# Three blocks of the second merge gate moved ahead of a recurrence's readout, and the readout's quarters queued on TensorE behind named products

## The chip, the cores and the metric

One core of one Trainium2 chip runs the whole kernel in one launch. The metric is the device time of an execution in microseconds (us). Below, TensorE is PE (PEld its weight loads), VectorE is DVE, ScalarE is ACT, GpSimd is POOL and SyncE is SP; ACTq and SPq are the streams that ACT and SP issue their DMAs from.

## What is computed

One layer of a decoder trunk on 256 tokens of width 2048, in float32: a gated feed-forward layer, a mixer, and a second feed-forward layer, each between two norms. Only the mixer matters here. Cut down, with the names of the reference:

```
proj = u @ W_in                        # u: 256 x 2048; columns split into u_ssm, q, k/v, gates, g_a, g_b
bu   = einsum(u_ssm, B)                # 64 groups of 16 channels, 64 complex states each
x[t] = A * x[t-1] + bu[t]              # a linear recurrence over the tokens
y    = Re(C x) + D u_ssm               # its readout
y_A  = (gelu(y) @ W1) * sigmoid(gelu(y) @ W2)
y_B  = NSA(q, k, v) @ W_o              # attention: compressed, selected and windowed branch
h    = h + post((sigmoid(g_a) * y_A + sigmoid(g_b) * y_B) @ W_out)
```

## The kernel before

All large products run through one routine, `block`. It makes a 256 x 512 piece of a product in two PSUM accumulators (`acc`, one for each half `t` of the tokens; two pairs exist). The weights come as a stream of items of 512 KB (two slices of 128 rows by 512 columns), loaded by SP's DMAs into `raw`, and each item is split by ACT (L88, the high part `hi`) and DVE (L89, the low part `lo`), at most four items ahead of their use. For each slice and each half, three matmuls follow: hi x high part of the activations (L185), lo x high (L186), hi x low (L187). A block with 2048 rows has 8 items and 96 products. After each item a block calls `tick`, which by `pump` takes one entry off the list `background` and traces it there, so that other work is woven between the products.

The order on each engine is that in which the tile framework's scheduler puts the traced instructions when the kernel is built: among those that can go it prefers the earlier traced one. On the chip each engine works through its own list in that order, and waits where an operand isn't there. Buffers that share a tag (`wk`, thirteen of 128 x 512; `xp`, four PSUM tiles; `tab`, two; `four`, four) are handed out in the order in which the trace asks for them.

The mixer (L635 on) runs, in this order: two blocks for the recurrence's input (transposed into `urel`); a block for keys, one for values, one for the compressed branch's inputs; three narrower blocks for the queries (twice 384 columns, then 304 with the attention's gates, L769); the four blocks of the gate g_b in the order of `GATE_ORDER` (L969), whose sigmoids go by ACT (L963) and SP's DMAs to `sig_dram`, but for the last; then, four times, a block of g_a and two half-length blocks on `yth`/`ytl` (L983 to L990); then the attention's output product (L1011, from `qs`) and W_out.

The recurrence advances four tokens a step, 64 steps. `s5_in` (L685) makes its inputs on PE; `scan` (L693) does the steps on POOL, four instructions each (L698 to L701), each needing the one before it; `s5_out` (L705) reads the states out on PE, for two of eight channel groups at a time a quarter (two calls, 48 matmuls, L713), each call with a table of 768 KB loaded by ACT's DMA queue (L682). The readout needs the states of all 64 steps. `s5_gelu` (L718) takes a quarter through ACT and DVE (L721, L730 to L734), four PE transposes (L226) and on to `yth`/`ytl` (L726, L727). These entries go onto `background` in this order: eight `s5_in`, sixteen `scan` of four steps, and for each quarter two `s5_out` and one `s5_gelu`. The ticks of the key, value and compressed blocks (8 each) take the first 24, and those of the query blocks the rest. When the query blocks are traced, what is left of the list is pumped (L781), the recurrence's pool `ssm` is closed, and the attention's pool `nsa` is opened in its place: its first DMAs (`tb` L788, `pos` L795, `w2c` L797, from ACT's queue) go there. The attention puts 57 entries on the list (L943 to L956), which the ticks from the first block of g_b on take.

Of the kernel before, what the change touches and what calls it, by code (L numbers as in the profile page):

```python
# [12 lines left out]
AF = mybir.ActivationFunctionType  # L13
# [7 lines left out]
NT = 2  # L21
KD = D // 128
# [10 lines left out]
ACC_BUFS = 4  # L33
LAG = 3
GATE_ORDER = (1, 2, 3, 0)
OPENING = [(0, 0), 1, 2, (0, 1), (1, 0), 3, (0, 2), (1, 1), 4, (0, 3), (1, 2), (1, 3)]
ORDER = {3: 1, 4: 2, 5: 3}
MAGIC = 12582912.0
# [66 lines left out]
def body(tc, a):  # L105
    from contextlib import ExitStack, nullcontext

    nc = tc.nc
    V, S, G, T = nc.vector, nc.scalar, nc.gpsimd, nc.tensor
# [9 lines left out]
    def work(dt=F32):  # L119
        return wk.tile([128, 512], dt, name="wk", tag="wk")  # L120
# [42 lines left out]
    nc.scalar.dma_start(gains, a["gains"])  # L163
    for x in OPENING:
        if isinstance(x, tuple):
# [4 lines left out]
    background = []  # L170

    def pump(n=1):
        for _ in range(n):
            if background:
                background.pop(0)()

    def block(lhs, nk, width=512, tick=None, held=0, between=None, behind=None, lag=0):
        acc = [ps.tile([128, 512], F32, name="acc", tag="acc") for _ in range(NT)]

        def products(parts, kk, t):  # L180
            wh, wl = parts
            for k in range(wh.shape[1]):
                lh, ll = lhs(t, kk + k)
                o = acc[t][:, :width]
                T.matmul(o, lh, wh[:, k, :], start=kk + k == 0, stop=False)  # L185
                T.matmul(o, lh, wl[:, k, :], start=False, stop=False)  # L186
                T.matmul(o, ll, wh[:, k, :], start=False, stop=kk + k == nk - 1)  # L187

        kk = 0
        kept = []  # L190
        late = []
        while kk < nk:
            parts = stream.next()
            products(parts, kk, 0)
            if kk < nk - held:
                late.append((parts, kk))
                if len(late) > lag:
                    products(*late.pop(0), 1)
            else:
                kept.append((parts, kk))  # L200
                if late:
                    products(*late.pop(0), 1)
            kk += parts[0].shape[1]
            if tick is not None:
                tick(kk)
        for x in late:
            products(*x, 1)
        if held:
            if between is not None:
                between(acc)  # L210
            for n, (parts, k0) in enumerate(kept):
                ins = behind(n) if behind is not None else None
                with tc.issue_after(ins) if ins is not None else nullcontext():
                    products(parts, k0, 1)
        return acc
# [7 lines left out]
    def transpose4(src, cols=128, n=4):  # L223
        p = xp.tile([128, n, 128], F32, name="xp", tag="xp")
        for k in range(n):
            last_transpose[0] = T.transpose(p[:, k, :], src[:, k * cols:(k + 1) * cols], ident).ins  # L226
        return p

    last_transpose = [None]


    act_h = [None] * NT
# [399 lines left out]
    sig_dram = dp.tile([256, D - 512], F32, name="sig")  # L632


    def mixer(name, rr, gen, post, last):  # L635
# [31 lines left out]
        for b in range(2):  # L667
            acc = acc0 if b == 0 else block(act, KD)
            for t in range(NT):
                p = transpose4(natural(acc, t))  # L670
                for q in range(4):
                    x = p[32 * q:32 * q + 32].rearrange("p c (n j) -> p c j n", j=4)
                    for j in range(4):
                        o = urel[32 * j:32 * j + 32, 4 * b:4 * b + 4, q, 32 * t:32 * t + 32]
# [5 lines left out]
        def table(src, n):  # L680
            w = sm.tile([128, 1536], F32, name="tab", tag="tab", bufs=2)
            nc.scalar.dma_start(w[:, :n], src)  # L682
            return w
# [9 lines left out]
        def scan(n0, n1):  # L693
            for n in range(n0, n1):
                w = sm.tile([128, 2, 2, 32], F32, name="sc", tag="sc", bufs=2)
                x = st8[:, :, :, n]
                y = st8[:, :, :, n + 1]
                G.tensor_tensor(w[:, 0], x, a4r2, op=ALU.mult)  # L698
                G.tensor_tensor(w[:, 1], x[:, ::-1], a4i2, op=ALU.mult)  # L699
                G.tensor_tensor(y, y, w[:, 0], op=ALU.add)  # L700
                G.tensor_tensor(y, y, w[:, 1], op=ALU.add)  # L701
# [3 lines left out]
        def s5_out(ct):  # L705
            tab = table(out_dram[ct], 1536).rearrange("p (r q k) -> p r q k", r=3, q=4)
            if ct % 2 == 0:
                yps.append(xp.tile([128, 2, 2, 128], F32, name="xp", tag="xp"))
            for qh in range(2):
                for r in range(3):  # L710
                    for q2 in range(2):
                        q = 2 * qh + q2
                        T.matmul(yps[-1][64 * q2:64 * q2 + 64, ct % 2, qh, :],  # L713
                                 st8[:, r, 4 * ct + q, 0:64] if r < 2 else urel[:, ct, q, :],
                                 tab[:, r, q, :], start=r == 0, stop=r == 2, tile_position=(0, 64 * q2))


        def s5_gelu(cp2):  # L718
            yp = yps.pop(0)
            yw, y2 = work(), work()  # L720
            S.activation(yw, yp.rearrange("p a b (i c) -> p i a b c", i=4), AF.Copy)  # L721
            gelu2(yw, y2)
            p = transpose4(yw).rearrange("p i (q n) -> p i q n", q=2)
            ks = slice(2 * cp2, 2 * cp2 + 2)
            oh, ol = (x[:, ks].rearrange("p q (n i) -> p i q n", i=4) for x in (yth, ytl))
            S.activation(oh, p, AF.Copy, scale=0.5)  # L726
            V.scalar_tensor_tensor(ol, p, 0.5, oh.bitcast(F32), op0=ALU.mult, op1=ALU.subtract)  # L727

        def gelu2(y, t):
            S.activation(t, y, AF.Square)  # L730
            V.tensor_scalar(t, t, GELU_C * 0.044715, GELU_C, op0=ALU.mult, op1=ALU.add)
            V.tensor_tensor(t, t, y, op=ALU.mult)
            S.activation(t, t, AF.Tanh)
            V.scalar_tensor_tensor(y, t, 1.0, y, op0=ALU.add, op1=ALU.mult)  # L734
# [2 lines left out]
            background.append(lambda ct=ct: s5_in(ct))  # L737
        for n0 in range(0, 64, 4):
            background.append(lambda n0=n0: scan(n0, n0 + 4))
        for ct in range(8):  # L740
            background.append(lambda ct=ct: s5_out(ct))
            if ct % 2:
                background.append(lambda ct=ct: s5_gelu(ct // 2))


        acc = block(act, KD, tick=tick)
# [21 lines left out]
        rh = [rr_half(rr(t), f"rh{t}") for t in range(NT)]  # L768
        for p0, np_, width in ((0, 3, 384), (3, 3, 384), (6, 2, 304)):  # L769
            acc = block(act, KD, width=width, tick=tick)  # L770
            for t in range(NT):
                p = transpose4(natural(acc, t, 128 * np_), n=np_)
                for hf in range(2):
                    own, other = (slice(64 * o, 64 * o + 64) for o in (hf, 1 - hf))
                    qh, ql = (qs[o, p0:p0 + np_, hf, t * 128:(t + 1) * 128] for o in (own, other))
                    S.activation(qh, p[own], AF.Copy, scale=-0.125)
                    V.scalar_tensor_tensor(ql, p[own], -0.125, qh.bitcast(F32), op0=ALU.mult, op1=ALU.subtract)
                if width == 304:
                    S.activation(gates[t], acc[t][:, 256:304], AF.Tanh, scale=rh[t])
                    V.tensor_scalar(gates[t], gates[t], 0.5, 0.5, op0=ALU.mult, op1=ALU.add)  # L780
        pump(len(background))  # L781
        ssm.__exit__(None, None, None)

# [172 lines left out]
                background.append(lambda u=units[i - 1]: values(*u))  # L956


        def gate(ab_acc):
            sg = []  # L960
            for t in range(NT):
                sg.append(work())
                S.activation(sg[t], ab_acc[t], AF.Tanh, scale=rh[t])  # L963
            return sg

        def sig_place(nb, t):
            return sig_dram[t * 128:(t + 1) * 128, (nb - 1) * 512:nb * 512]

        for nb in GATE_ORDER:  # L969
            sg_b = gate(block(act, KD, tick=tick))  # L970
            if nb:
                for t in range(NT):
                    nc.sync.dma_start(sig_place(nb, t), sg_b[t])

        def ylhs(t, kk):
            return yth[:, kk, t * 128:(t + 1) * 128], ytl[:, kk, t * 128:(t + 1) * 128]
# [5 lines left out]
        for nb in range(NBD):  # L982
            sg = gate(block(act, KD, tick=tick))  # L983
# [20 lines left out]
        for nb in range(NBD):  # L1004
            if nb:
                sg_b = []
# [3 lines left out]
            sg, w2 = sg_b, ya[nb]  # L1010
# [17 lines left out]
    def rr_half(r, nm):  # L1028
        h = cp.tile([128, 1], F32, name=nm, tag=nm)
        V.tensor_scalar(h, r, 0.5, None, op0=ALU.mult)  # L1030
        return h
# [57 lines left out]
def layout(i):  # L1089
# [19 lines left out]
    d["w_qg"] = _tiles(np.concatenate([q[:, 768:], gn], axis=1), 304)  # L1109
    d["w_gate_b"] = _tiles(np.concatenate([gb[:, nb * 512:(nb + 1) * 512] for nb in GATE_ORDER], axis=1))  # L1110
    wo = f["nsa_w_o"].reshape(16, 64, D)[heads].reshape(1024, D)
# [33 lines left out]
```

## Time and profile before

| | |
|---|---|
| median of 3 runs | 2211.38 us (2211.06 to 2211.67) |
| the profiled execution | 2210.69 us |
| its span in the trace | 2208.9 us |
| PE busy | 2145.2 us, 97% |
| DVE, ACT, POOL busy | 54%, 45%, 11% |
| mean granted PE clock | 0.987 of full |

Times in the trace are us from the start of the span. "Idle before" is the time in which the engine sat idle ahead of an instruction, with what released it behind the arrow. Matmuls are pipelined, so that the pace of a run of products is read from the distance of their starts, not from the length of one. POOL's records are rough: the last step of the recurrence is recorded as ending some 1.4 us after the matmul that needed it had begun.

### The profile page before, as it was taken

Reading aid. Unit: us, or ns where it says so; the run is one execution under the profiler, and the core shown is the slowest. Engines: PE = TensorE matmul, PEld = TensorE weight load, DVE = VectorE, ACT = ScalarE, POOL = GpSimd, SP = SyncE. Lnnn points to the kernel's source line nnn. Section 1 sums busy time; section 2 is a strip of 40 time slices with the busy share of each in tenths; the row PEclk is TensorE's granted clock in tenths of the full one; section 3 lists DMA queues with packets and bytes.
Section 4 is the critical chain, followed back from the end, with each engine's and each line's share of the span. In section 5 each row is a group of like instructions: output and inputs, shape, how many; then the busy total and the mean of one; then the engine's idle time right before and its main releaser. Section 6 shows DMA issues by size and latency. Waiting matters only on the chain.

```text
span 2208.9 us, 27461 instructions
## 1 busy us (share of the span) xinstructions
PE 2145.2 (97%) x10246; PEld 1772.9 (80%) x10246; DVE 1197.5 (54%) x1674; ACT 998.5 (45%) x1347; POOL 249.1 (11%) x494
## 2 busy tenths in 40 slices
PE   8999999999999999659999999999999999999998
PEld 7888888888888888647877788888888888888887
DVE  7877745544444654324555546574455444544444
ACT  6444444444444654324455444473444444444442
POOL 1222210000000006931044200000000000000000
PEclk9999999999999999869999999999999999999999
DMA  8777766666666766437533456575656665666664
GB/s 290 255 235 234 228 190 191 190 190 195 197 199 218 249 210 195 127 116 267 191 127 130 145 191 223 195 261 190 190 190 190 191 191 190 190 191 199 198 215 161
DMA packets 137141, 437.60 MB, mean 198 GB/s; under 512 B 14880, under 2 KB 27312, under 8 KB 136880
## 3 DMA queue, kind: packets, MB, share of 16 engines
q1 hardware_dynamic: 117504, 403.10, 56.4%
q10 hardware_dynamic: 19504, 32.75, 4.4%
q8 instruction: 80, 1.31, 0.2%
q14 instruction: 53, 0.43, 0.1%
HBM read 417.42 MB, written 21.52 MB: 199 GB/s over the span
## 4 chain that ended last, share of the span: by engine, by line
PE 93%; POOL 5%; issue 1%; DMA 0%; ACT 0%; ACTq 0%; DVE 0%; DVEq 0%; SPq 0%; POOLq 0%
PE acc L185 29%; PE acc L187 29%; PE acc L186 29%; PE xp L226 2%; POOL sc L698 1%; POOL sc L699 1%; POOL st L701 1%; POOL st L700 1%; PE xp L937 1%; PE xp L713 1%; PE xp L690 1%; PE xp L925 1%; PE xp L826 0%; PE xp L901 0%; PE xp L931 0%
## 5 line engine op out<-in xcount | busy, mean ns | idle before, releaser
L89 DVE TENSOR_TENSOR lo<-raw,hi 128x1024 fp32r<-128x1024 f32 (+2 forms) x702 | 854.6, 1219 | 844.8 <-ACT hi L88 836.7
L88 ACT ACTIVATE hi<-raw 128x1024 fp32r<-128x1024 f32 (+2 forms) x702 | 737.5, 1052 | 993.3 <-PE acc L187 933.0
L185 PE MATMUL acc<-hi,ah 128*128 128x512 f32 (+2 forms) x1968 | 764.2, 390 | 7.6 <-ACT wk L657 6.2
L186 PE MATMUL acc<-lo,ah 128*128 128x512 f32 (+2 forms) x1968 | 763.1, 388 | 0.0
L187 PE MATMUL acc<-hi,al 128*128 128x512 f32 (+2 forms) x1968 | 762.8, 388 | 0.0
L185 PEld LDWEIGHTS acc<-hi,ah 128*128 128x128 f32 x1968 | 370.9, 189 | 83.1 <-ACT wk L657 6.7
L187 PEld LDWEIGHTS acc<-hi,al 128*128 128x128 f32 x1968 | 370.9, 188 | 74.2 <-issue 1.3
L186 PEld LDWEIGHTS acc<-lo,ah 128*128 128x128 f32 x1968 | 371.2, 189 | 72.3 <-issue 1.3
L187 PE MATMUL acc<-hi,hT 128*128 128x512 f32 x648 | 252.1, 389 | 0.0
L186 PE MATMUL acc<-lo,hT 128*128 128x512 f32 x648 | 252.1, 389 | 0.0
L185 PE MATMUL acc<-hi,hT 128*128 128x512 f32 x648 | 251.9, 389 | 0.0
L185 PEld LDWEIGHTS acc<-hi,hT 128*128 128x128 f32 x648 | 121.7, 188 | 25.2
L187 PEld LDWEIGHTS acc<-hi,hT 128*128 128x128 f32 x648 | 121.7, 188 | 25.2
L186 PEld LDWEIGHTS acc<-lo,hT 128*128 128x128 f32 x648 | 121.7, 188 | 25.1
L302 POOL TENSOR_TENSOR rpc<-rpc,mhalf 128x1 f32<-128x1 f32 x2 | 1.1, 548 | 719.5 <-DVE rpc L300 719.5
L588 POOL COPY hz<-hs 32x128 f32<-32x128 f32 (+3 forms) x128 | 58.7, 459 | 183.3 <-DVE hs L583 176.3
L912 POOL TENSOR_SCALAR four<-four,sx 128x128 f32<-128x128 f32 (+1 forms) x64 | 59.2, 943 | 123.7 <-ACT four L907 65.2
L226 PE MATMUL xp<-ident,wk 128*128 128x128 f32 x368 | 51.0, 278 | 9.0 <-DMA wk<-in_x 4.9
L226 PEld LDWEIGHTS xp<-ident,wk 128*128 128x128 f32 x368 | 44.3, 143 | 16.0 <-issue 9.1
L302 POOL TENSOR_TENSOR rpa<-rpa,mhalf 128x1 f32<-128x1 f32 x2 | 1.1, 554 | 468.5 <-DVE rpa L300 468.5
L713 PE MATMUL xp<-tab,st 128*64 128x128 f32 x128 | 12.5, 327 | 39.6 <-POOL st L701 39.6
L185 PE MATMUL acc<-hi,yth 128*128 128x512 f32 x128 | 50.3, 393 | 0.0
(264 smaller groups left out, 1544.0 us busy)
## 6 DMA issues: line engine op xcount, KB each, us to landing
raw<-in_ffn_gu SPq DMA_DIRECT2D x352, 512.0 KB, 3.6
raw<-in_ffn_d SPq DMA_DIRECT2D x176, 512.0 KB, 3.6
raw<-in_w_ya SPq DMA_DIRECT2D x64, 512.0 KB, 3.5
raw<-in_w_in SPq DMA_DIRECT2D x40, 512.0 KB, 4.6
raw<-in_w_gate_b SPq DMA_DIRECT2D x32, 512.0 KB, 4.1
raw<-in_w_out SPq DMA_DIRECT2D x32, 512.0 KB, 4.3
raw<-in_w_o SPq DMA_DIRECT2D x16, 512.0 KB, 4.2
tab<-s5out ACTq DMA_DIRECT2D x8, 768.0 KB, 5.5
```

The lines of the kernel that those rows point to most:

```text
L88: self.rounded.append(nc.scalar.activation(h, r, AF.Copy).ins)
L89: nc.vector.tensor_tensor(l, r, h.bitcast(F32), op=ALU.subtract)
L185: T.matmul(o, lh, wh[:, k, :], start=kk + k == 0, stop=False)
L186: T.matmul(o, lh, wl[:, k, :], start=False, stop=False)
L187: T.matmul(o, ll, wh[:, k, :], start=False, stop=kk + k == nk - 1)
L226: last_transpose[0] = T.transpose(p[:, k, :], src[:, k * cols:(k + 1) * cols], ident).ins
L588: G.tensor_copy(hq[32 * j:32 * j + 32, q, j:, :], hs[32 * q:32 * q + 32, 0:4 - j, :])
L690: T.matmul(sp[:, r, q, :], bt[:, r, q, :], urel[:, ct, q, :], start=True, stop=True)
L698: G.tensor_tensor(w[:, 0], x, a4r2, op=ALU.mult)
L699: G.tensor_tensor(w[:, 1], x[:, ::-1], a4i2, op=ALU.mult)
L713: T.matmul(yps[-1][64 * q2:64 * q2 + 64, ct % 2, qh, :], st8[:, r, 4 * ct + q, 0:64] if r < 2 else urel[:, ct, q, :], tab[:, r, q, :], sta ...
L912: G.tensor_scalar(P[:, b, :nk], P[:, b, :nk], sx[:, 2 + b:3 + b], None, op0=ALU.mult)
```

## The change

A constant `EARLY_GATES = 3` is added. `gate` and `sig_place` are moved up, unaltered, and a routine `gate_b` does a block of g_b with its sigmoid and its stores. The first three blocks of g_b (nb = 1, 2, 3) are traced right behind the query blocks, ahead of the last pump and the closing of `ssm`; the fourth (nb = 0) stays where all four stood, and is the first whose ticks take the attention's entries. The weights' order in the stream is the same.

The readout isn't put on the list together with the scan. Ahead of the third block of g_b the list is emptied, and eight entries go onto it: readout of a quarter, gelu of that quarter, four times. The third block's eight ticks take them. Each readout is traced under `issue_after(last_product[0])`: its PE instructions may not stand on PE ahead of the latest L187 product traced by then (`block` now keeps it in `last_product`), that is the last product of items 1, 3, 5 and 7 of the third block.

```diff
+EARLY_GATES = 3
@@ block, products
-                T.matmul(o, ll, wh[:, k, :], start=False, stop=kk + k == nk - 1)
+                last_product[0] = T.matmul(o, ll, wh[:, k, :], start=False, stop=kk + k == nk - 1).ins
@@ mixer, background of the recurrence
-        for ct in range(8):
-            background.append(lambda ct=ct: s5_out(ct))
-            if ct % 2:
-                background.append(lambda ct=ct: s5_gelu(ct // 2))
+        def readout(c2):
+            with tc.issue_after(last_product[0]):
+                for ct in (2 * c2, 2 * c2 + 1):
+                    s5_out(ct)
@@ mixer, behind the query blocks
+        def gate_b(nb):
+            sg = gate(block(act, KD, tick=tick))
+            if nb:
+                for t in range(NT):
+                    nc.sync.dma_start(sig_place(nb, t), sg[t])
+            return sg
+
+        for i, nb in enumerate(GATE_ORDER[:EARLY_GATES]):
+            if i == EARLY_GATES - 1:
+                pump(len(background))
+                for c2 in range(4):
+                    background.append(lambda c2=c2: readout(c2))
+                    background.append(lambda c2=c2: s5_gelu(c2))
+            gate_b(nb)
         pump(len(background))
         ssm.__exit__(None, None, None)
@@ mixer, behind the attention's entries
-        for nb in GATE_ORDER:
-            sg_b = gate(block(act, KD, tick=tick))
-            if nb:
-                for t in range(NT):
-                    nc.sync.dma_start(sig_place(nb, t), sg_b[t])
+        for nb in GATE_ORDER[EARLY_GATES:]:
+            sg_b = gate_b(nb)
```

## Rows read from the trace of the kernel before

**Rows 1.** The page: busy time by engine, PE's granted clock in 40 slices of 55.2 us (tenths of full speed), and the engines' shares of the chain that ended last.
```profile
PE 2145.2 (97%) x10246; PEld 1772.9 (80%) x10246; DVE 1197.5 (54%) x1674; ACT 998.5 (45%) x1347; POOL 249.1 (11%) x494
...
PEclk9999999999999999869999999999999999999999
...
PE 93%; POOL 5%; issue 1%; DMA 0%; ACT 0%; ACTq 0%; DVE 0%; DVEq 0%; SPq 0%; POOLq 0%
```

**Rows 2.** PE's waits of the whole span (what waited, for whom: total us, times, longest us); the two that are left out belong to the start of the kernel (4.9) and to a weight split (1.4).
```profile
PE xp L713 <- POOL st L701: 39.6, 1, 39.6
PE acc L185 <- ACT wk L657: 6.2, 2, 4.4
...
PE xp L226 <- DVE wk L734: 4.0, 1, 4.0
```

**Rows 3.** The timeline of PE from the second query block's last product on, merged (start, us, instruction, idle before): the first three readout quarters (L713), transposes (L226), the third query block (L185). Between 975.91 and 981.30 stand 27 recorded products.
```profile
920.04 0.34 PE L187 MATMUL acc<-hi,al 128*128 128x384 f32 x1
959.97 1.12 PE L713 MATMUL xp<-tab,st 128*64 128x128 f32 x8 [39.59 <-POOL st L701]
...
968.32 1.09 PE L226 MATMUL xp<-ident,wk 128*128 128x128 f32 x4 [4.03 <-DVE wk L734]
969.33 1.12 PE L713 MATMUL xp<-tab,st 128*64 128x128 f32 x8
...
975.91 0.41 PE L185 MATMUL acc<-hi,ah 128*128 128x304 f32 x1 [1.83 <-ACT wk L657]
...
981.30 0.60 PE L226 MATMUL xp<-ident,wk 128*128 128x128 f32 x4
981.83 0.66 PE L713 MATMUL xp<-tab,st 128*64 128x128 f32 x8
...
984.61 0.87 PE L226 MATMUL xp<-ident,wk 128*128 128x128 f32 x6
```

**Rows 4.** Windows of that stretch and behind it: busy us of PE, PEld, DVE, ACT, POOL, then the granted clock, the DMA share and GB/s.
```profile
960.00:980.00 20.00, 14.14 (x118) 13.36 (x119) 4.71 (x7) 5.75 (x9) 1.31 (x4) 0.67 0.47 158
1000.00:1005.00 5.00, 2.16 (x5) 1.78 (x6) 1.49 (x4) 3.31 (x8) 0.00 (x0) 0.56 1.06 354
```

**Rows 5.** Starts of PE's products: two of 512 columns with 36 steps between them, two of 304 columns with 13 steps between them, and two of 512 columns next to each other in the first g_b block.
```profile
1083.15 0.40 PE L185 MATMUL acc<-hi,ah 128*128 128x512 f32 x1
...
1091.33 0.39 PE L185 MATMUL acc<-hi,ah 128*128 128x512 f32 x1
...
988.10 0.30 PE L187 MATMUL acc<-hi,al 128*128 128x304 f32 x1
...
989.91 0.30 PE L185 MATMUL acc<-hi,ah 128*128 128x304 f32 x1
...
1006.42 0.63 PE L187 MATMUL acc<-hi,al 128*128 128x512 f32 x1
1006.85 0.63 PE L185 MATMUL acc<-hi,ah 128*128 128x512 f32 x1
```

**Rows 6.** Windows for the last instruction of a scan step alone (L701 on POOL): its busy us and, behind x, how many steps; then the granted clock, the DMA share and GB/s. The scan begins at 842, the second query block ends at 920.2.
```profile
842.00:886.00 44.00, 9.80 (x20) 1.00 0.58 187
842.00:920.20 78.20, 15.53 (x36) 1.00 0.57 179
903.60:920.20 16.60, 2.87 (x8) 1.00 0.54 158
```

**Rows 7.** The timelines of POOL and of DVE: a scan instruction beside a weight split (L89), and the scan's last two steps, with DVE idle.
```profile
868.29 1.42 POOL L701 TENSOR_TENSOR st<-st,sc 128x64 f32<-128x64 f32 x1
...
868.26 1.22 DVE L89 TENSOR_TENSOR lo<-raw,hi 128x1024 fp32r<-128x1024 f32 x1 [0.90 <-ACT hi L88]
...
959.56 0.35 POOL L701 TENSOR_TENSOR st<-st,sc 128x64 f32<-128x64 f32 x1
...
961.03 0.35 POOL L701 TENSOR_TENSOR st<-st,sc 128x64 f32<-128x64 f32 x1
```

**Rows 8.** The sixteen DMAs that load the recurrence's tables (L682), us from issue to landing; and a window of what follows the readout (columns as in rows 4).
```profile
DMA to landing us min/median/max: 4.3/4.9/8.4
...
1000.00:1040.00 40.00, 37.16 (x171) 28.57 (x172) 19.90 (x24) 19.83 (x30) 4.85 (x2) 0.91 0.81 269
```

**Rows 9.** The timeline of ACT and of its DMA queue: the second quarter's gelu (L721, L730, L726; L733 is of the same form and length as L730) with the first query block's L657 behind its L730, and the second of the attention's first DMAs; and the group of the weight splits on ACT (busy us, mean ns of one).
```profile
974.13 0.60 ACT L721 ACTIVATE wk<-xp 128x512 f32<-128x512 f32 x1 [3.60 <-PE xp L713]
...
974.76 0.63 ACT L730 ACTIVATE wk<-wk 128x512 f32<-128x512 f32 x1
975.30 1.04 ACT L657 ACTIVATE wk<-acc,rna 128x384 f32<-128x384 f32 x2
...
981.98 1.11 ACT L726 ACTIVATE yth<-xp 128x512 fp32r<-128x512 f32 x1
...
997.41 4.22 ACTq L795 DMA_DIRECT2D pos<-in_cmp_pos  x1
...
L88 ACT ACTIVATE hi<-raw 128x1024 fp32r<-128x1024 f32 (+2 forms) x702 | 737.5, 1052 | 993.3 <-PE acc L187 933.0 <-issue 16.4 <-POOL hz L588 11.8
```

**Rows 10.** The attention's last result, the first product that reads the attention's results, and a window of the attention's busiest stretch (columns as in rows 4).
```profile
1255.59 0.29 DVE L941 TENSOR_TENSOR qs<-xp,qs 128x128 fp32r<-128x128 f32 x1 [0.38 <-ACT qs L940]
...
1335.53 0.39 PE L185 MATMUL acc<-hi,qs 128*128 128x512 f32 x1
...
1150.00:1200.00 50.00, 50.00 (x291) 38.02 (x287) 30.00 (x97) 27.43 (x69) 19.51 (x22) 1.00 0.36 127
```

More of the change, by code (lines that the diff above doesn't have):

```diff
@@ L229, in body @@
     last_transpose = [None]
+    last_product = [None]
     act_h = [None] * NT
@@ L780, in mixer, with gate, sig_place @@
                     V.tensor_scalar(gates[t], gates[t], 0.5, 0.5, op0=ALU.mult, op1=ALU.add)
+        def gate(ab_acc):
+            sg = []
+            for t in range(NT):
+                sg.append(work())
+                S.activation(sg[t], ab_acc[t], AF.Tanh, scale=rh[t])
+            return sg
+        def sig_place(nb, t):
+            return sig_dram[t * 128:(t + 1) * 128, (nb - 1) * 512:nb * 512]
+        def gate_b(nb):
+            sg = gate(block(act, KD, tick=tick))
+            if nb:
+                for t in range(NT):
+                    nc.sync.dma_start(sig_place(nb, t), sg[t])
+            return sg
+        for i, nb in enumerate(GATE_ORDER[:EARLY_GATES]):
[5 more added lines that the diff above has]
+            gate_b(nb)
         pump(len(background))
@@ L956, in mixer @@
                 background.append(lambda u=units[i - 1]: values(*u))
-        def gate(ab_acc):
-            sg = []
-            for t in range(NT):
[L962 to L967, printed above, removed]
-        for nb in GATE_ORDER:
-            sg_b = gate(block(act, KD, tick=tick))
-            if nb:
-                for t in range(NT):
-                    nc.sync.dma_start(sig_place(nb, t), sg_b[t])
+        for nb in GATE_ORDER[EARLY_GATES:]:
+            sg_b = gate_b(nb)
         def ylhs(t, kk):
```

## The prediction, made before the changed kernel was run

> **What bounds the kernel now.** I read the page first. PE is busy for 97% of the span, so that the kernel is the sum of PE's work and PE's waits; no other engine passes 54%. Its granted clock is lower in two slices in the middle, and the chain that ended last has 5% of POOL, an engine that is busy for only 11% [rows 1]. The list of PE's waits names the place: one wait of 39.6 us for the recurrence's last step on POOL, 6.2 us for ACT in two, 4.0 us for DVE in one; the rest is small and elsewhere [rows 2]. The timeline of PE puts these into one stretch behind the query blocks [rows 3]. The reader should see there that the 48 matmuls of the first readout quarter stand on PE right behind the second query block, while the third query block, which needs nothing of the recurrence, stands behind two quarters. It needs the accumulators of the first query block, these are emptied by ACT's L657, and that stands on ACT behind the first steps of the gelu of two quarters [rows 9], since the `wk` buffers are handed out in trace order. So what the third query block could have covered is locked behind the readout as well.
>
> **What the stretch costs.** From the end of the second query block (920.2: the last product starts at 920.04) PE idles 39.59 + 4.03 [rows 3] + 6.2 [rows 2] = 49.8 us. On top comes a granted clock of 0.67 in the window from 960 to 980 and of 0.56 at 1000 to 1005 [rows 4], so half speed (1.2 GHz) for part of them, after PE had been idle. What it costs I take from work of the same kind at both speeds. A quarter at full speed takes 2.78 us (the third: 981.83 to 984.61); the first took 4.32 (959.97 to 964.29, where the 4.03 us of waiting begin), the second 4.75 (969.33 to 974.08, where the 1.83 begin): 1.54 + 1.97. Four transposes took 1.01 instead of 0.53: 0.48 [rows 3]. A product of 512 columns takes (1091.33 - 1083.15) / 36 = 0.227 us, one of 304 columns (989.91 - 988.10) / 13 = 0.139 us [rows 5]; the 27 products from 975.91 to 981.30 [rows 3] took 5.39 instead of 3.75: 1.64. In the first g_b block some ten products took 0.43 [rows 5]: with a slow start, 2.2. Together 7.8 us. **The stretch holds 49.8 + 7.8 = 57.6 us that are not work.**
>
> **Part 1: three blocks go ahead.** They add nothing: the same 96 products each, in the same order of the stream. What they do is give PE work that needs no state of the recurrence: 96 x 0.227 = 21.8 us each. The third query block (96 x 0.139 = 13.4 us) is freed too, because the gelu no longer stands ahead of L657 on ACT. With the 16 transposes of the query blocks (at 0.53 / 4, 2.1 us) the first readout quarter, behind the third gate block's first item (12 products, 2.7 us), comes up on PE at 920.2 + 13.4 + 2.1 + 2 x 21.8 + 2.7 = **982.0 us** at the earliest.
>
> When is the recurrence done by then? Before, its last steps ran while DVE stood still, at 961.03 - 959.56 = 1.47 us each. Now DVE will be splitting weights all through, and that is dearer: a scan instruction of 0.35 us takes 1.42 when it meets an L89 of 1.22 [rows 7], and in the blocks of 512 columns 20 steps took 44 us, 2.2 each [rows 6]. By the row, 36 steps are done at 920.2 [rows 6], 28 remain, and 28 x 2.2 = 61.6 puts the end at 981.8 in POOL's records. These run 1.4 us late against PE's (the last step ends at 961.38, the matmul that needed it began at 959.97) [rows 3, 7]: 980.4. **The cover is nearly exact: 1.6 us to spare.** The fastest loaded pace (16.6 / 8 = 2.08) gives 977 and no wait; the slowest, with the count of a window of 22 us with ten steps one too high at its edges (22 / 9 = 2.44), gives 987 and a wait of 5 us, after which the clock falls as it did after 4.4 us of idling (2.2 us more). I take 0 for this wait, since the 512-wide blocks are the nearest rows, with 0 to 7 us as bounds.
>
> The Trainium skill (GPSIMD Engine Reference, 1. Specifications) states that GpSimd's SBUF interfaces are shared with VectorE, with contention for DVE instructions with two SBUF inputs, which L89 is; that speaks against this change. The trace agrees, at 1.42 against 0.35 us [rows 7]. Without such a rule the scan would be over at 960 as before, and the change would have 22 us to spare instead of 1.6; the sum would be the same.
>
> **Part 2: the quarters are spread over the third block.** PE's work in them is the same (4 x 2.78 us). What is new is what each can wait for. A quarter's tables need the buffers of the quarter before it: 768 KB each, 4.3 to 8.4 us to landing, median 4.9 [rows 8], issued from ACT's queue when half of the quarter before is done. Two items and four transposes lie between: the second quarter begins 2.8 + 5.4 + 0.5 = 8.7 us after the first, and its first table lands at some 1.4 + 0.6 + 4.9 = 6.9, at the longest 10.4, a wait of 1.7. For three quarters: 0 to 5 us; I take 1, since the tables now share the DMA engines with a full stream of weights. The third block moves 4.2 MB of weights and 4.7 MB of tables in 21.8 + 4 x 2.8 + 3 x 0.5 = 34.5 us, 258 GB/s, and the trace has 269 over 40 us [rows 8] and 354 over 5 [rows 4]: SP's weights don't fall behind. ACT has 8 x 1.05 of splits and 4 x 2.97 of gelu (0.60 + 2 x 0.63 + 1.11) [rows 9], 20 of 34.5 us; the sigmoids and the DMA issues fit beside them. The gelu of a quarter takes 4.0 us when nothing else runs (what the first transposes waited) [rows 3]; products now lie between, but ACT and DVE are also busy with splits: 0 to 2 us for each of four, I take 0.5 in all. Going back and forth between products and other matmuls: 0.5 us more than before.
>
> The sigmoid of the third block stands on ACT behind the last gelu's L730, because `wk` is handed out in order. Waiting for it are two accumulators, which the block after next needs 22 us later, and SP's stores with the weight loads behind them; up to five raw items and four split ones are ahead. Nothing.
>
> **Part 3: the attention starts later.** Its DMAs wait for the last quarter. The 4.2 us in which ACT sat on the issue of `pos` [rows 9] come again, but now behind the third block: no accumulators that PE needs at once hang on it, and PE has up to four split items (2.7 us each) in hand. Nothing, up to 2 us. The 57 entries have only 8 + 64 ticks. Before, `pos` was issued at 997.4 and the attention's last result stood at 1255.9, 258.5 us later; the product that reads it began at 1335.5 [rows 9, 10]. Now the last quarter ends at some 979.3 (the third block's start) + 19.1 (seven items) + 11.1 (four quarters) + 1.6 (transposes) = 1011.1, the attention at some 1270.2, and PE arrives at its output product at 1335.5 - 55.6 = 1280; the last heads are needed by the fourth item, 8 us later. The cover shrinks from 80 us to 10 (18 for the last heads), but it holds.
>
> **Sum.** 57.6 - (0 + 1 + 0.5 + 0.5) = 55.6 us. The profiled execution took 2210.69 (its span of 2208.9 and 1.8 around it), which gives 2155.1; it lies 0.7 under the median, which gives 2211.38 - 55.6 = 2155.8: **2156 us.**
>
> **The rivals.**
>
> *The scan outlasts the cover.* For it: the margin is 1.6 us of 62. Then PE waits at the third block for POOL for 3 to 6 us, and the clock takes 2 more: 2159 to 2164.
>
> *The readout's chain is slower than its spacing.* Each quarter waits for tables and gelu, the scheduler puts later quarters into the fourth block, the attention ends behind 1288, and PE waits at its output product. The price is what the attention is late, less the 18 us; a chain of 20 us a quarter instead of 8.7 delays the last quarter by 3 x 11.3 = 34 and costs 16, less with waits of only a few us at the quarters: 2159 to 2172.
>
> *It doesn't do what it says.* `issue_after` sets only the earliest place on PE. If something that the readout holds still locks PE's next work behind it on ACT, only the wait for POOL goes: 2211.4 - 39.6 = 2172.
>
> *Slower.* The attention becomes the bound of the mixer. Its 57 entries share their ticks with the g_a blocks, where ACT and DVE have the sigmoid products besides. It decides from an end of the attention 18 us behind its forecast, and the change loses from 18 + 55.6 = 74 us on: 258.5 us would have to become 332 or more. At 340 us the time is 2219. Against it: DVE is at 60% and ACT at 55% in its busiest stretch [rows 10], and what the g_a blocks add is small.
>
> **Chances.** Forecast (2152 to 2159) 0.60; scan outlasts 0.16; chain 0.12; not what it says 0.07; slower 0.03, and 0.02 for about the same. The range reaches from 2151, a stretch with nothing new and some 2 us of order that falls well elsewhere, to 2172, which leaves out less than 0.1. Changes under 0.2% (4.4 us) can't be told from none in this kernel: faster 0.95, same 0.02, slower 0.03.
>
> **What would show it.** Right: PE's waits have no line for POOL above 2 us; the granted clock is 1.0 from 900 to 1020; the quarters are a few us apart, with products between, and begin at some 982; the scan's steps take 2.2 us up to its end at about 981; the attention's last result comes before 1280. Wrong: a wait L713 <- POOL of over 3 us (the cover's pace is off), L713 <- DMA or L226 <- DVE of over 3 us in sum (part 2), a wait of the first product on `qs` (part 3), or L185 <- ACT L657 still there (the lock).

## The result and the profile after

| | before | changed |
|---|---|---|
| median | 2211.53 us | 2154.77 us (2154.32 to 2155.35) |
| ratio to before, 95% interval | | 0.9742 [0.9725, 0.9759] |
| span of the profiled execution | 2208.9 us | 2153.0 us |
| mean granted PE clock | 0.987 | 0.999 |

The change saves 55.9 us of the profiled executions' span (forecast: 55.6) and 56.8 us between the medians, 2.6% of the time. Lines of the changed kernel are numbered a little higher: the readout is L716 (L713 before), the last instruction of a scan step L704 (L701), the DVE split L91 (L89), the accumulator's L657 is L660, the attention's last result L970 (L941), the transposes L228 (L226), ACT's split L90 (L88), and the three products L187 to L189 (L185 to L187).

The page of the changed kernel, to be held against [rows 1]:

```profile
PE 2137.8 (99%) x10246; PEld 1765.6 (82%) x10246; DVE 1201.0 (56%) x1674; ACT 998.4 (46%) x1347; POOL 273.2 (13%) x494
...
PEclk9999999999999999999999999999999999999999
```

PE has the same 10246 instructions. Its busy time is 7.4 us less: the granted clock is full in every slice, and the half clock had added this to the same instructions (7.8 in the prediction). And the span less the busy time fell from 63.7 to 15.2 us. POOL is busy 24 us longer with the same 494 instructions: the scan is now loaded to its end. All of PE's waits of the whole span, against [rows 2]:

```profile
PE xp L228 <- DMA wk<-in_x: 5.2, 2, 4.9
PE acc L187 <- ACT hi L90: 1.6, 2, 1.4
PE xp L716 <- POOL st L704: 0.9, 1, 0.9
```

What is left is the start of the kernel (4.9 of the 5.2 us), a weight split and 0.9 us for the scan. The timeline of PE, merged, around the first readout quarter and ahead of the second to the fourth, against [rows 3]:

```profile
981.80 0.39 PE L189 MATMUL acc<-hi,al 128*128 128x512 f32 x1
983.11 0.66 PE L716 MATMUL xp<-tab,st 128*64 128x128 f32 x8 [0.92 <-POOL st L704]
...
994.64 0.60 PE L228 MATMUL xp<-ident,wk 128*128 128x128 f32 x4
995.16 0.66 PE L716 MATMUL xp<-tab,st 128*64 128x128 f32 x8
...
1008.37 0.66 PE L716 MATMUL xp<-tab,st 128*64 128x128 f32 x8
...
1020.66 0.66 PE L716 MATMUL xp<-tab,st 128*64 128x128 f32 x8
```

The reader should see two things. The first quarter came up at 983.11 - 0.92 = 982.2 (forecast 982.0), with the scan some 1 us behind it (forecast: 1.6 ahead). And the quarters are 12 to 13 us apart, not 8.7; between them PE does products without a wait. The windows for L704 show the scan's pace under the gate blocks (behind x the steps), against [rows 6]:

```profile
920.00:940.00 20.00, 3.66 (x9) 1.00 0.75 241
940.00:960.00 20.00, 5.13 (x9) 1.00 0.64 213
960.00:980.00 20.00, 4.77 (x8) 1.00 0.64 213
```

26 steps in 60 us are 2.3 us a step; in the last two rows of [rows 7] it was 1.47 with DVE idle.

The attention's last result and the first product that reads it, as first and last start of their groups (the sixteen L970; L187 on `qs`), against [rows 10]:

```profile
L970 DVE TENSOR_TENSOR qs<-xp,qs x16: 269/284/292, 1140.3 to 1273.8; 128x128 fp32r<-128x128 f32 x16
...
L187 PE MATMUL acc<-hi,qs x64: 389/389/476, 1279.6 to 1325.1; 128*128 128x512 f32 x64
```

The attention ends 5.5 us ahead of its reader (80 before; forecast 10).

### The profile page after: what moved, and what is told of

Its sections match the earlier page's. It is cut to its first block, busy times and chain, and to the rows that moved or that the text cites. A ratio compares the mean times of both kernels' runs of the same rounds, so it can differ in the third digit from the quotient of the medians.

```text
span 2153.0 us, 27454 instructions
## 1 busy us (share of the span) xinstructions
PE 2137.8 (99%) x10246; PEld 1765.6 (82%) x10246; DVE 1201.0 (56%) x1674; ACT 998.4 (46%) x1347; POOL 273.2 (13%) x494
## 4 chain that ended last, share of the span: by engine, by line
PE 91%; POOL 6%; issue 1%; DMA 1%; DVE 1%; ACT 0%; DVEq 0%; SPq 0%; ACTq 0%; POOLq 0%
PE acc L187 28%; PE acc L188 28%; PE acc L189 28%; PE xp L228 2%; POOL sc L701 2%; POOL st L704 2%; POOL st L703 1%; POOL sc L702 1%; PE xp L966 1%; PE xp L693 1%; PE xp L954 1%; PE xp L716 1%; PE xp L855 0%; DMA s5out<-gb 0%; PE xp L930 0%
## 5 line engine op out<-in xcount | busy, mean ns | idle before, releaser
L91 DVE TENSOR_TENSOR lo<-raw,hi 128x1024 fp32r<-128x1024 f32 (+2 forms) x702 | 858.8, 1224 | 822.9 <-ACT hi L90 813.2
L90 ACT ACTIVATE hi<-raw 128x1024 fp32r<-128x1024 f32 (+2 forms) x702 | 737.5, 1052 | 970.8 <-PE acc L189 907.4
L187 PE MATMUL acc<-hi,ah 128*128 128x512 f32 (+2 forms) x1968 | 762.7, 389 | 1.6 <-ACT hi L90 1.6
L189 PE MATMUL acc<-hi,al 128*128 128x512 f32 (+2 forms) x1968 | 761.3, 387 | 0.0
L187 PEld LDWEIGHTS acc<-hi,ah 128*128 128x128 f32 x1968 | 369.8, 188 | 77.7 <-issue 3.6
L189 PEld LDWEIGHTS acc<-hi,al 128*128 128x128 f32 x1968 | 369.8, 188 | 72.8 <-issue 0.2
L189 PE MATMUL acc<-hi,hT 128*128 128x512 f32 x648 | 252.1, 389 | 0.0
L187 PE MATMUL acc<-hi,hT 128*128 128x512 f32 x648 | 251.9, 389 | 0.0
L189 PEld LDWEIGHTS acc<-hi,hT 128*128 128x128 f32 x648 | 121.6, 188 | 25.3
L187 PEld LDWEIGHTS acc<-hi,hT 128*128 128x128 f32 x648 | 121.6, 188 | 25.1
L941 POOL TENSOR_SCALAR four<-four,sx 128x128 f32<-128x128 f32 (+1 forms) x64 | 59.3, 944 | 122.7 <-ACT four L936 59.3
L228 PE MATMUL xp<-ident,wk 128*128 128x128 f32 x368 | 51.1, 276 | 5.2 <-DMA wk<-in_x 5.2
L228 PEld LDWEIGHTS xp<-ident,wk 128*128 128x128 f32 x368 | 44.4, 143 | 12.3 <-issue 4.9
L187 PE MATMUL acc<-hi,yth 128*128 128x512 f32 x128 | 50.6, 395 | 0.0
L189 PE MATMUL acc<-hi,ytl 128*128 128x512 f32 x128 | 50.5, 395 | 0.0
```

Of the source, the lines that this page charges most:

```text
L90: self.rounded.append(nc.scalar.activation(h, r, AF.Copy).ins)
L91: nc.vector.tensor_tensor(l, r, h.bitcast(F32), op=ALU.subtract)
L189: last_product[0] = T.matmul(o, ll, wh[:, k, :], start=False, stop=kk + k == nk - 1).ins
L941: G.tensor_scalar(P[:, b, :nk], P[:, b, :nk], sx[:, 2 + b:3 + b], None, op0=ALU.mult)
```

## The experiments

The theory to be tested: the 57.6 us hang on the scan's late end and on the lock of the `wk` order, and on nothing else; the three g_b blocks are cover, counted in PE time; the scan's pace, which the cover has to outlast, is set by DVE's splits. The main rivals: the moving of the gates, or the naming of products, does the work by itself; or part of the loss stands on its own.

### One part alone: the gates moved, the readout left on the list

```diff
-        def readout(c2): ...                       # and its entries ahead of the third block
+        for ct in range(8):                        # directly behind the scan's entries, as before
+            background.append(lambda ct=ct: s5_out(ct))
+            if ct % 2:
+                background.append(lambda ct=ct: s5_gelu(ct // 2))
```

> The three g_b blocks are moved up, but the readout and gelu entries stay on the list directly behind the scan, as before. My theory (the query blocks' and gates' accumulators hang on wk buffers that are handed out behind the gelu, so that whatever stands behind the readout in the trace is locked): the first quarter stands behind the second query block again, PE waits some 39.6 us for POOL, and the time is 2211 +- 4 us. Rival (moving the gates up is enough, since they need nothing of the recurrence and can fill the wait): 2155 to 2175 us.

Measured: 2213.25 us, ratio 1.0006 [0.9997, 1.0015]. PE's waits are those of [rows 2] again:

```profile
PE xp L716 <- POOL st L704: 39.5, 1, 39.5
PE acc L187 <- ACT wk L660: 6.1, 2, 4.3
...
PE xp L228 <- DVE wk L737: 4.0, 1, 4.0
```

Three blocks that need nothing of the recurrence stood earlier in the program and moved nothing. They were traced ahead of the attention, but still behind the readout, whose entries the query blocks' ticks take, and the waits for ACT's L660 (L657 before) are there as before. Moving the gates is not enough; where the readout is traced decides.

### The other part alone: the readout traced last, no gate moved

The kernel before, with the readout and the gelu traced right behind the third query block.

```diff
-        for ct in range(8):
-            background.append(lambda ct=ct: s5_out(ct)) ...
         pump(len(background))
+        for c2 in range(4):
+            s5_out(2 * c2)
+            s5_out(2 * c2 + 1)
+            s5_gelu(c2)
         ssm.__exit__(None, None, None)
```

> The kernel before, with the readout and the gelu taken off the list and traced right behind the third query block; no g_b block is moved. This takes away the lock (the first query block's L657 no longer stands behind the gelu) and nothing else. My theory: PE does the third query block first and comes to the first quarter at some 936 us, with 21 scan steps to go: a wait of some 30 us, 2185 to 2200. Rival (the lock was the whole cause: once it is gone the scheduler fills the wait with g_b blocks, which need nothing of the recurrence): 2155 to 2170.

Measured: 2182.17 us, ratio 0.9864 [0.9849, 0.9878]. The timeline of PE:

```profile
941.31 0.39 PE L187 MATMUL acc<-hi,al 128*128 128x512 f32 x1
...
967.51 1.12 PE L713 MATMUL xp<-tab,st 128*64 128x128 f32 x8 [25.82 <-POOL st L701]
```

Taking the lock away is worth some 30 us: the third query block, and the first 30 recorded products of the first g_b block, which the scheduler put ahead by itself, now stand before the wait; the waits for L657 and L734 are gone. The rest, 2182.2 - 2154.8 = 27 us, is a wait of 25.8 us and the clock behind it, which needs more cover or an earlier end of the scan. The time is 3 us below the range that I gave; the 30 products (30 x 0.227 = 6.8 us), which I had left to the rival, are more than that.

### The same with half of the scan

As the last kernel, but 32 of the 64 scan steps are left out (`range(0, 32, 4)`).

> The kernel before with the readout traced behind the third query block (no lock) and with 32 of the 64 scan steps left out; no g_b block is moved and nothing is tied to a product. The scan ends at some 907 us, well ahead of the place that the trace order gives to the first quarter (some 936). My theory (the lost 57.6 us come from the late scan and the lock alone; the g_b blocks that the change moves are cover and nothing else): no wait of PE for POOL, a granted clock of 1.0 throughout, 2153 to 2158 us. Rival (part of the loss stands by itself: ACT's issue of pos, the gelu ahead of the transposes, and moving the gates is what hides it): 2160 to 2172 us.

Measured: 2154.36 us, ratio 0.9741 [0.9724, 0.9757], the time of the changed kernel, without any of its moved gates. The kernel before took 2211.78 us beside it: 57.4 us more, against the 57.6 us that the prediction counted. PE's waits, complete:

```profile
PE xp L226 <- DMA wk<-in_x: 5.0, 1, 5.0
PE acc L185 <- ACT hi L88: 1.4, 1, 1.4
```

So no loss of a size that can be measured stood by itself. Where the scan ends in time and the order holds no lock, the g_b blocks may stay where they were.

### Half of the scan in the kernel before, as it was

```diff
-        for n0 in range(0, 64, 4):
+        for n0 in range(0, 32, 4):
```

> The kernel before, with 32 of the 64 scan steps left out. The scan would then end at some 842 + 32 x 2.2 = 912 us, ahead of the place of the first quarter. My theory (all that the stretch lost came from the late end of the scan, the waits for ACT and DVE and the clock with it): 2152 to 2160 us, like the changed kernel, with at most the 4.4 us of ACT's issue of pos left. Rival (the scan's wait is one loss among several that stand by themselves): only the 39.6 us go, 2172 us.

Measured: 2173.98 us, ratio 0.9828 [0.9813, 0.9843]: near the rival's number, but not for its reason, and my expectation failed. With eight entries fewer on the list the readout's entries moved forward by eight ticks as well, and the first quarter now stood inside the first query block, with a wait for POOL of its own:

```profile
894.88 0.34 PE L187 MATMUL acc<-hi,al 128*128 128x384 f32 x1
907.09 1.12 PE L713 MATMUL xp<-tab,st 128*64 128x128 f32 x8 [11.87 <-POOL st L701]
```

To it came 2.6 and 2.2 us of waits for ACT's L657. The run changed two things at once and couldn't tell the theories apart; the experiment above, which holds the readout's place, does. What made the scheduler choose just this place was not tried.

### Two blocks of cover instead of three

```diff
-EARLY_GATES = 3
+EARLY_GATES = 2
```

> Two g_b blocks go ahead instead of three, the readout's quarters stand in the second. My theory (the cover is counted in PE time, and three blocks are just enough): the first quarter comes up 21.8 us earlier, at some 960.4 us, with 10 of the 64 scan steps to go; three more of them at 2.2 us while weights are still split ahead, the others at 1.47 while DVE stands still, 16.9 us; PE waits 15 to 17 us for POOL, the clock falls for some 3.5 us of time: 2170 to 2175 us. Rival 1 (the scan keeps its loaded pace of 2.2 us whatever DVE does): a wait of 22 us, 2178 to 2182. Rival 2 (it is the placing behind named products that counts, not how much stands ahead): 2153 to 2157.

Measured: 2171.51 us, ratio 0.9817 [0.9802, 0.9831]. PE's wait, and a window of it (busy us of PE, PEld, DVE, ACT, POOL, granted clock, DMA share, GB/s):

```profile
975.62 1.12 PE L716 MATMUL xp<-tab,st 128*64 128x128 f32 x8 [14.82 <-POOL st L704]
...
960.00:980.00 20.00, 5.18 (x50) 4.72 (x50) 2.44 (x2) 1.06 (x1) 15.39 (x42) 0.66 0.34 97
```

A block less (21.8 us of PE) costs 16.7: the wait grew by 13.9 to 14.8 and not by 21.8, because the scan runs faster in it: 11 steps in the 16 us from 960.4 to the start of the last one at 976.7, with DVE nearly still (2.44 of 20 us busy). The clock adds the rest. Both rivals are out.

### Two blocks, and DVE's splits left out

For the third query block and the g_b blocks the low part isn't made; the high part stands in for it, so that PE, ACT and the DMAs do what they did. The edit, cut down:

```diff
+        if i in self.whole:            # the items of w_qg and w_gate_b
+            self.rounded.append(nc.scalar.activation(h, self.raw.pop(i), AF.Copy).ins)
+            self.parts[i] = (h, h)     # no V.tensor_tensor(l, r, h, subtract)
```

> Two g_b blocks ahead, and DVE's part of the weight split (the low part) left out for the third query block and the four g_b blocks: the high part is used in its place, so that PE does the same matmuls, ACT and the DMAs do the same work, and only DVE's 40 two-operand instructions are gone. It leaves the low parts of these weights out of the result. My theory (it is DVE's splits that slow the scan from 1.47 to 2.2 us a step): from some 912 us on the scan goes at 1.5, the last 32 steps take 48 us, it is done at 960, when the first quarter comes up; PE waits 0 to 2 us, 2153 to 2158 us. Rival (the scan is slow because PE, the DMAs or ACT are busy): the pace stays at 2.2, PE waits 15 us as with two blocks and the splits, 2170 to 2175.

Measured: 2154.54 us, ratio 0.9740 [0.9724, 0.9757]; PE has no wait for POOL. The windows for the last instruction of a scan step (here L715):

```profile
920.00:940.00 20.00, 4.67 (x13) 1.00 0.79 255
940.00:960.00 20.00, 4.99 (x14) 1.00 0.64 210
```

27 steps in 40 us are 1.48 us a step, with PE at full clock and the DMAs at 210 to 255 GB/s; the kernel with two blocks and the splits has 18 steps in the same 40 us, and so has the changed kernel. All engines in these 40 us (columns as above), first with the splits, then without:

```profile
920.00:960.00 40.00, 40.00 (x223) 35.78 (x222) 23.87 (x28) 23.70 (x34) 37.26 (x72) 1.00 0.70 220
...
920.00:960.00 40.00, 40.00 (x226) 35.39 (x226) 4.32 (x10) 23.10 (x34) 35.72 (x107) 1.00 0.72 232
```

PE, ACT and the DMAs are as busy as before, and DVE alone has less to do, 4.32 us instead of 23.87. In the whole kernel 40 splits are gone. They are what slows the scan, and without them two blocks are cover enough.

### Without the names

```diff
-            with tc.issue_after(last_product[0]):
+            with nullcontext():
```

> As the change, but the readout is traced without being tied to a product of the third block. My theory: the trace order alone already puts it behind the first two g_b blocks, since products traced earlier go first; the naming moves it by an item or two, and the wait for POOL grows from 0.9 to 3 to 6 us with 2 us of clock: 2155 to 2163 us. Rival (the naming carries the change: without it the scheduler puts the readout as far ahead as its own idea of the scan's end allows): a wait of over 15 us, 2170 to 2212.

Measured: 2153.36 us, ratio 0.9734 [0.9718, 0.9750].

```profile
981.38 0.39 PE L189 MATMUL acc<-hi,al 128*128 128x512 f32 x1
981.70 0.66 PE L716 MATMUL xp<-tab,st 128*64 128x128 f32 x8
```

The first quarter stood at 981.70, where the named one came up at 982.2, and PE didn't wait there. PE's order is that of the changed kernel: the first quarter stands behind 204 products of the g_b blocks in both, and 38, 43 and 39 recorded products lie behind the first three quarters in both. So the trace order alone does it, and the naming is worth nothing here. My own expectation, a wait of 3 to 6 us and 2155 us or more, was wrong as well as the rival. In this run the scan was done some 2.5 us earlier in POOL's records than in the changed kernel's (its last step begins at 982.7 instead of 985.2), which is more than the wait of 0.9 us. It ended as early in the next two runs (982.7 and 982.5), whose gate blocks stand beside the scan in the same way; why the changed kernel's trace is the late one stays open.

### Each quarter an item later

```diff
                 pump(len(background))
+                background.append(lambda: None)
                 for c2 in range(4):
```

> As the change, but each quarter one item later (behind items 2, 4, 6 and 8 of the third block). My theory: PE's wait of 0.9 us for POOL goes, the attention ends some 2.7 us later and still ahead of its reader: 2153 to 2155 us, a gain of 0 to 1 us that the runs may not tell from none. Rival (the scan runs a step later still because its last steps are now loaded too, and the attention's cover of 5.5 us is used up): 2156 to 2160.

Measured: 2154.01 us, ratio 0.9737 [0.9723, 0.9752]. The wait of 0.9 us is gone, and the gain isn't measurable. Since the scan ended 2.5 us earlier here too, the wait might have been gone without the later place.

### Four blocks of cover

```diff
-EARLY_GATES = 3
+EARLY_GATES = 4                        # and sg_b = gate_b(nb) in the early loop
```

> All four g_b blocks go ahead, the readout's quarters stand in the fourth, and the attention's entries are first taken by the g_a blocks. PE's cover for the scan grows by 21.8 us, so its wait of 0.9 us goes. My theory (the attention's results become late: in the changed kernel they stood at 1274.1 and were first read at 1279.6, the last heads 8 us later; now they come 21.8 us later and PE's work up to their reader is the same): PE waits 8 to 16 us at the output product, 2161 to 2172 us. Rival (the attention is paced by PE's order and catches up): 2152 to 2157.

Measured: 2154.11 us, ratio 0.9737 [0.9723, 0.9752]: the rival's time came true, and my expectation of a wait was wrong, though the attention did become late. First and last starts, as above:

```profile
L970 DVE TENSOR_TENSOR qs<-xp,qs x16: 271/285/292, 1160.0 to 1293.7; 128x128 fp32r<-128x128 f32 x16
...
L187 PE MATMUL acc<-hi,qs x64: 388/390/481, 1270.5 to 1324.5; 128*128 128x512 f32 x64
```

The attention's last result begins 23 us *behind* the first product that reads its results, and PE has no wait for it: the scheduler put products of the heads that were done between the attention's last matmuls, the first already at 1270.5, and the last ones end at the same time as before.

## Why the prediction was right

**What bounds the kernel, and the 57.6 us.** Right, and shown: with the scan halved and the lock gone the kernel before loses 57.4 us. The terms: PE's time without work fell by 48.5 us (the prediction counted 49.8 in the stretch, and 0.9 for the scan is new), PE's busy time, which holds the clock's part, by 7.4 us against 7.8. The kernels without a long wait differ in PE's busy time by up to 1.4 us among themselves (2137.7 to 2139.1), so that this term agrees within its noise.

**The lock.** It was read from one place in ACT's order [rows 9], and it turned out to be the larger half: 30 of 57 us go when the readout is only traced later. The three gates are worth the other 27, and nothing at all while the readout is traced ahead of them. That it is `wk` by which the order locks was read and not tested by itself: no run gave L657 buffers of its own. The trace of before has the same order a second time, where L657 follows on the fourth quarter's L730, and L730 comes late because ACT sits on the issue of `pos`:

```profile
1001.69 0.63 ACT L730 ACTIVATE wk<-wk 128x512 f32<-128x512 f32 x1 [4.15 <-issue]
...
1002.22 1.40 ACT L657 ACTIVATE wk<-acc,rna 128x384 f32<-128x384 f32 x3
...
1002.84 0.80 PE L185 MATMUL acc<-hi,ah 128*128 128x512 f32 x1 [4.36 <-ACT wk L657]
```

So 4.4 of the 6.2 us for L657 hang on the issue of `pos` as well. In the changed kernel ACT sits on it again, for 4.10 us from 1023.98 on, and PE doesn't wait, as part 3 of the prediction said.

**The cover and the scan.** Right in its place (982.2 against 982.0) and within 3 us in the scan's end. I took 2.2 us a step and this trace has 2.3, so that the margin of 1.6 us became a wait of 0.9, within the bounds of 0 to 7. In the runs with no names, with an item more and with four blocks it is 27 steps in the 60 us from 920 to 980, 2.2 a step, and no wait: the margin is smaller than what one trace differs from the next. The contention that I took from one pair of rows [rows 7] is now shown by an intervention. The Trainium skill (SBUF — State Buffer, SBUF: two separate sides) describes it as an exclusive lock: of a DVE instruction with two SBUF inputs and a GpSimd instruction that reads SBUF, the one that started first holds the shared ports throughout. The trace agrees in the pair of [rows 7], where the scan instruction began 0.03 us behind an L89 of 1.22 us and took 1.42 instead of 0.35.

**The quarters' spacing: wrong in size, without a price.** I took the spacing from the named items (8.7 us). The schedule gave 12 to 13: a quarter stands on PE behind the transposes of the one before, and the scheduler left 8.8 to 10.3 us (38 to 45 recorded products) between a quarter and its transposes where the gelu needs 4. That `xp` is handed out in order would explain the first; it was not tested. The names don't set the spacing, since the order without them is the same. So the chain ran into the fourth block and the last quarter ended at 1023.4, not 1011. The tables were then always there in time, and the waits for tables and gelu, for which I had put 1.5 us, were zero; the 0.5 us for going back and forth had no row behind it and can't be told from nothing here. The rival on the slow chain was right that the chain runs into the fourth block, and wrong about the waits and the price.

**The attention.** Its end at 1274.1 was forecast as 1270, and PE's arrival at 1279.6 as 1280. The first hit is luck in part, for two misses nearly cancel: the last quarter ended 12 us later than forecast, and from the issue of `pos` (1023.98) to its last result the attention took 250.1 us and not 258.5. What was wrong besides is the price behind it: I held that PE would wait from an end some 18 us later on, and four blocks of cover showed an end 20 us later (1294.0) without a wait. So the change was further from becoming slower by this path than I said; how far was not tried.

**The sum.** 57.6 - 2 = 55.6 us forecast, 55.9 measured: the new terms that I put at 2 us were 0.9 for the scan, for which I had taken 0, and nothing that can be told from none for the tables, the gelu and the going back and forth, for which I had taken 2. That the sum came so close is luck in these small terms; the 57.6 us that carry it are not.

## What to carry to other kernels

A wait on the critical engine is not only as long as the late producer: look at what stands behind the waiting instruction and why, and follow it through buffers that are handed out in trace order, because work that needs nothing of the producer can be locked there, and moving more such work up gains nothing while it stays behind the lock. Count cover at the producer's pace under the load that the cover itself brings (2.2 to 2.3 us a step here, not the 1.47 seen in the old wait), and test the parts of such a change by themselves: here tracing the readout later gave 30 us, the cover 27 and the pinning to named instructions nothing. An experiment that takes work away must hold the order fixed, or it tests two things.

## What the runs showed of the hardware that I had not expected

POOL lost a third of its pace for as long as DVE split weights: 27 steps in 40 us without the splits, 18 with them. So simple a subtraction on DVE, 40 instructions with 49 us of DVE's time in all, is worth as much as a whole block of cover (2171.5 against 2154.5 us). And a wait of PE costs more than its length: PE's busy time was 3.6 us longer than in the changed kernel with a wait of 14.8 us (granted clock 0.66 from 960 to 980), 3.2 us longer with one of 25.8 us, and 7.4 us longer in the kernel before, with one of 39.6 us and three of 4.4 us or less behind it. It didn't grow with the length of the wait from 14.8 to 25.8 us.
